# One more group of seven products in three FFN stages, and one pool for split weights and activations

## The chip, the core and the metric

The kernel runs on one core of a Trainium2 chip. The core has five engines with a queue each: TensorE (PE in the profile) multiplies matrices into PSUM, VectorE (DVE) and ScalarE (ACT) do elementwise work, GpSimd (POOL) does small work and issues some transfers, and SyncE (SP) issues the other transfers. An engine works its queue in order and waits on semaphores for the others. The metric is the device time of one execution in microseconds.

## The reference

The reference is a two-layer encoder over 256 tokens of width 1024, in float32. Each layer is a half FFN, an attention mixer and a second half FFN:

```
def swiglu(h, w_gate, w_up, w_down):
    return (jax.nn.silu(h @ w_gate) * (h @ w_up)) @ w_down
...
x = x + 0.5 * swiglu(rms_norm(x, ffn1_norm[l]), ffn1_w_gate[l], ffn1_w_up[l], ffn1_w_down[l])
h = rms_norm(x, mix_norm[l])
...                                # windowed and differential attention, output projection
x = x + 0.5 * swiglu(rms_norm(x, ffn2_norm[l]), ffn2_w_gate[l], ffn2_w_up[l], ffn2_w_down[l])
```

The FFN width is 2816. A last RMSNorm follows the second layer. This case is about the four FFNs, called stages 1 to 4 here.

## The kernel before, in words

**Precision.** Every float32 operand of a large product is split into a high part, rounded to the matmul's type, and a low part, the difference. A product is then three matmuls: high by high, low by high, high by low. ScalarE casts the high part and VectorE subtracts to get the low part, for weights (`emit_split`, L175) and for activations (`split`, L506). One weight step is a block of 512 rows by 512 columns, 1 MB, that lands in a `raw` buffer (6 of them); it is split in two halves of 128 x 1024 elements each, and each half fills two buffers tagged `w`.

**An FFN stage** (`ffn`, L567). The width 2816 is done in groups 0 to 4 of 512 columns and a tail of 256. A plain group multiplies the normed tokens `xs` with 512 columns of the gate and the up matrix (8 row blocks, 2 token blocks, 2 matrices, 3 matmuls: 96 matmuls of 128 x 512), then SiLU and the product give h (`gate`, `hidden`). The h of a group is transposed in the next group (`turn`, eight transposes, `hT`), where its two products with the down matrix (`down`, 24 matmuls each) also stand. Four PSUM banks hold the down sums (`accs`) from group 1 on; the other four go round among gate, up, transposes and products.

**Groups of seven products** (`by_seven`, L599). In groups 2, 3 and 4 of every stage, the gate and up products over two row halves and two token blocks are treated as a 2 x 2 by 2 x 2 block product and done with seven block products in place of eight (Strassen's scheme in Winograd's form). Each is 12 matmuls, so 84 in place of 96. They use sums of token blocks and sums of weight blocks. The token sums are made once a stage by `Norm.make_sums` (L332) from float copies of the normed tokens, `xg`, which `Norm.copies` (L322) writes from PSUM. It yields after each of four sums; each is an addition on VectorE (`tmp`), a cast on ScalarE and a subtraction on VectorE (tiles `q`, three times, and `v`). Two weight sums are accumulated by transfers that POOL issues (`gather`), two are made by VectorE (`plus`, two additions each on `raw`). The seven products, in their order in the code, are m1, m7, p2, p3, p5, p6 and p4; m7, p3, p5 and p6 take the token sums, and p3 takes the one that is made last. VectorE combines the products in seven operations on `tmp`, and two more make h.

**The order of the work.** Engines run in the order of the code in all of the FFN. Loads and splits of weights are put in ahead of their use by `ahead` (L211), called from `weights` (L232) and in the middle of each step by `Split.part`. The lookahead is HALVES = 6 halves, from 14 `w` buffers; activations have a pool of their own of 14 buffers (`s4`). In `make_sums` before, the sums are made in group 1, one after the gate, one after each of the two up steps, and one between the two down products.

**Around a stage.** The norm of the next stage begins while the last products of the one before still run; `Residual.late` (L557) finishes its statistics (`stats`: `ms`, then r by POOL, then `hr`) and makes the copies. In stage 1 `take_x` (L409) does that. `attention_constants` (L475), one transpose, a dozen small operations on VectorE and one exponential on ScalarE, is put in at the head of group 3 of stage 1 by `aside`; `final_gain` (L969), one transfer and one memset, at the head of group 3 of stage 4.

Of the kernel before, what the change touches and what calls it, by code (L numbers as in the profile page):

```python
# [21 lines left out]
NGRP = FF // 512  # L22
# [5 lines left out]
AHEAD = 10  # L28
N_RAW, N_W = 6, 14
N_S4 = 14  # L30
SEVEN = (2, 3, 4)


@with_exitstack
def trunk(ctx: ExitStack, tc: tile.TileContext, x, n1, g1, u1, d1, nm, w_in, sink,
# [124 lines left out]
    class Split:  # L160
# [5 lines left out]
        def part(self, k, c=slice(None), h=None):  # L166

            if h is None:
                h, k = divmod(k, 2)
            if h and not self.held:  # L170
                self.held = True
                ahead(2 * self.i + 1 + HALVES)
            return [t[:, k, c] for t in self.parts[h]]

    def emit_split(i, j):  # L175
# [4 lines left out]
        shape = (P, 8, P) if s.n == 256 else (P, 2, 512)  # L180
        hi, lo = [wp.tile(list(shape), F32R, tag="w", bufs=N_W, name=nm_("w")) for _ in range(2)]
        loaded[i].parts.append((hi, lo))
# [24 lines left out]

    HALVES = N_W // 2 - 1
    at = dict(use=0, dma=2, prep=2, split=4)
# [22 lines left out]
    def weights(less=0, held=False):  # L232

        i = at["use"]
        at["use"] += 1
        if i > 1:
            ahead(2 * i + HALVES - less)
        w = loaded[i]
        w.held = held
        return w  # L240

    for l in range(DEPTH):
        def ffn_specs(wg, wu, wd):
            down = lambda g, h: plain(wd[l], h * 512, 512, 4 * g, 4)
            for k0 in (0, 4):
                specs.extend(plain(w[l], 0, 512, k0, 4) for w in (wg, wu))
            for g in range(1, NGRP):
                downs = [down(g - 1, h) for h in range(2)]
                if g in SEVEN:
# [11 lines left out]

        ffn_specs(g1, u1, d1)
        wi = w_in[l]
# [19 lines left out]
        fine.update(range(mixed + 2, len(specs)))  # L283
        ffn_specs(g2, u2, d2)

# [3 lines left out]
    class Norm:  # L289


        def __init__(self, g0, sums=len(SEVEN) > 0):
# [39 lines left out]
        def make_sums(self):  # L332
# [5 lines left out]
            def make(x, y, op):  # L338
# [7 lines left out]
                return v  # L346

            s1 = make(b1, t1, ALU.subtract)
            yield
            s2 = make(s1, t0, ALU.add)  # L350
            yield
            make(t1, t0, ALU.subtract)
            yield
# [55 lines left out]
    def take_x(k):  # L409
# [14 lines left out]
        elif k == 2:  # L424
            ahead(7)
            for t in range(2):
                for h in range(2):
                    norm.squares(t, h * 512, 512)
            norm.stats()
            norm.copies()  # L430
            constants()
# [110 lines left out]
    class Residual:  # L542
# [14 lines left out]
        def late(self, k):  # L557
# [5 lines left out]
            elif k == 2:  # L563
                self.nxt.stats()
                self.nxt.copies()

    def ffn(norm, aside=None, before=None, final=False):  # L567
        def silu(out_, acc, t):
            act.activation(out_, acc, AF.Silu, scale=norm.r[:, t:t + 1])
# [28 lines left out]

        def by_seven(h, g):  # L599

# [64 lines left out]
        tokens(us, norm.xs, weights(), 4)  # L665
        h = hidden(g, us)
        for n in range(1, NGRP):
            sums = norm.make_sums() if n + 1 == min(SEVEN, default=0) else iter(())
            if n == 3 and aside is not None:
                aside()  # L670
            if n in SEVEN:
                h = by_seven(h, n)
                continue
            gs = [bank(), bank()]
            tokens(gs, norm.xs, weights(), 0)
            hT = turn(h, 2)
            tokens(gs, norm.xs, weights(), 4)
            g = gate(gs)
# [41 lines left out]
    def ffn_close(parts, nxt):  # L720
# [6 lines left out]
        tail(1)  # L727
        ahead(2 * at["use"] - 2 + HALVES)
        group(1, [(1, t) for t in range(2)])
# [326 lines left out]
```

## Time and profile before

| what | value |
|---|---|
| median of the runs shown | 944.5 us (944.03, 944.5, 947.19) |
| profiled execution, its own time | 946.16 us |
| its span, first to last instruction | 944.4 us |
| mean granted TensorE clock | 0.993 |
| PE busy | 924.9 us, 98% |
| DVE busy | 762.2 us, 81% |
| ACT busy | 582.2 us, 62% |
| POOL busy | 53.6 us, 6% |
| matmuls of 128 x 512 over a split weight, tokens in s | 2718, mean 394 ns from start to end |
| weight splits on DVE, 128 x 1024 | 336, 396.7 us |
| weight casts on ACT, 128 x 1024 | 336, 340.1 us |
| weight additions on DVE | 48, 56.5 us |
| accumulating transfers from POOL | 24 of 1 MB, median 10.7 us from issue to landing |

Matmuls overlap, so a mean of 394 ns is not the distance from one to the next. In the names of the profile, `w` is a split weight, `raw` a landed one, `s` an activation, `q` and `v` token sums in the FFN (and other tiles in attention), `tmp` the results of products and of SiLU. An arrow names who ended an idle time. All instructions carry the line of one helper, so groups are told apart by their tiles.

### The profile page before, as it was taken

Reading aid. Unit: us, or ns where it says so; the run is one execution under the profiler, and the core shown is the slowest. Engines: PE = TensorE matmul, PEld = TensorE weight load, DVE = VectorE, ACT = ScalarE, POOL = GpSimd, SP = SyncE. Lnnn points to the kernel's source line nnn. Section 1 sums busy time; section 2 is a strip of 40 time slices with the busy share of each in tenths; the row PEclk is TensorE's granted clock in tenths of the full one; section 3 lists DMA queues with packets and bytes.
Section 4 is the critical chain, followed back from the end, with each engine's and each line's share of the span. In section 5 each row is a group of like instructions: output and inputs, shape, how many; then the busy total and the mean of one; then the engine's idle time right before and its main releaser. Section 6 shows DMA issues by size and latency. Waiting matters only on the chain.

```text
span 944.4 us, 12947 instructions
## 1 busy us (share of the span) xinstructions
PE 924.9 (98%) x4796; PEld 783.5 (83%) x4796; DVE 762.2 (81%) x1066; ACT 582.2 (62%) x901; POOL 53.6 (6%) x73
## 2 busy tenths in 40 slices
PE   8999899999999999999999999999999999999997
PEld 6788688899898888887888888878999888888876
DVE  6679999869955678999866799996796556799993
ACT  6756576467735756675575566665676475575662
POOL 0500010000000000000000010000000000010001
PEclk9999899999999999999999999999999999999999
DMA  9986797836424875897658498886652348499821
GB/s 336 345 222 182 218 277 255 271 120 194 134 90 134 233 213 141 263 295 265 239 178 235 122 278 223 259 296 195 194 161 90 130 157 249 103 286 268 254 93 45
DMA packets 110895, 194.59 MB, mean 206 GB/s; under 512 B 3566, under 2 KB 31280, under 8 KB 110832
## 3 DMA queue, kind: packets, MB, share of 16 engines
q1 hardware_dynamic: 96816, 167.27, 52.2%
q0 software_dynamic: 12928, 25.46, 15.1%
q10 hardware_dynamic: 1088, 1.05, 0.3%
q8 instruction: 37, 0.61, 0.3%
q14 instruction: 26, 0.21, 0.1%
HBM read 192.71 MB, written 1.05 MB: 205 GB/s over the span
## 4 chain that ended last, share of the span: by engine, by line
PE 83%; DVE 7%; DMA 5%; issue 2%; ACT 2%; ACTq 0%; DVEq 0%; POOLq 0%; POOL 0%
PE ps L50 83%; DVE w L50 5%; DMA raw<-in_ffn_w_up_dram 3%; DVE tmp L50 1%; ACT w L50 1%; DMA raw<-in_ffn_w_gate_dram 1%; DMA xk<-in_x_dram 1%; DVE s L50 1%; DVE raw L50 0%; ACT s L50 0%; ACT junk L50 0%; ACT tmp L50 0%; ACT L50 0%; ACTq L50 0%; DVE xk L50 0%
## 5 line engine op out<-in xcount | busy, mean ns | idle before, releaser
L50 PE MATMUL ps<-w,s 128*128 128x512 f32 (+1 forms) x2754 | 645.4, 392 | 7.1 <-DVE tmp L50 3.5
L50 PEld LDWEIGHTS ps<-w,s 128*128 128x128 f32 x2754 | 514.0, 189 | 115.2 <-DVE tmp L50 4.8
L50 DVE TENSOR_TENSOR w<-raw,w 128x1024 fp32r<-128x1024 f32 (+1 forms) x440 | 464.1, 1094 | 86.9 <-ACT w L50 84.1
L50 ACT CAST w<-raw 128x1024 fp32r<-128x1024 f32 (+1 forms) x440 | 399.1, 949 | 189.7 <-PE ps L50 97.1
L50 PE MATMUL ps<-w,q 128*128 128x512 f32 x432 | 101.9, 389 | 0.0
L50 PEld LDWEIGHTS ps<-w,q 128*128 128x128 f32 x432 | 81.1, 188 | 16.8
L50 PE MATMUL ps<-s,w 128*128 128x256 f32 x672 | 84.0, 285 | 0.0
L50 PEld LDWEIGHTS ps<-s,w 128*128 128x128 f32 x672 | 81.7, 192 | 1.1
L50 DVE TENSOR_TENSOR raw<-raw,raw 128x1024 f32<-128x1024 f32 x48 | 56.5, 1218 | 0.0
L50 POOL DMA_DIRECT2D raw<-in_ffn_w_up_dram x24 | 31.0, 1293 | 364.4 <-DVE tmp L50 157.2
L50 DVE TENSOR_TENSOR s<-ps,s 128x512 fp32r<-128x512 f32 x48 | 31.0, 685 | 18.1 <-ACT s L50 18.1
L50 ACT ACTIVATE s<-ps,gcol 128x256 fp32r<-128x256 f32 (+1 forms) x80 | 31.3, 476 | 20.7 <-PE ps L50 20.7
L50 ACT CAST s<-ps 128x512 fp32r<-128x512 f32 x48 | 26.1, 594 | 28.1 <-PE ps L50 28.1
L50 PE MATMUL ps<-ident,s 128*128 128x128 f32 x304 | 39.9, 273 | 1.7 <-DVE s L50 1.7
L50 PEld LDWEIGHTS ps<-ident,s 128*128 128x128 f32 x304 | 35.0, 141 | 6.9 <-ACT w L50 1.8
L50 ACT ACTIVATE s<-s,negm 128x256 f32<-128x256 f32 x64 | 31.8, 500 | 6.6 <-DVE negm L50 6.6
L50 ACT ACTIVATE tmp<-tmp,r 128x512 f32<-128x512 f32 x24 | 17.3, 722 | 29.2 <-DVE tmp L50 29.2
L50 PE MATMUL ps<-w,v 128*128 128x512 f32 x144 | 34.6, 389 | 0.0
L50 PEld LDWEIGHTS ps<-w,v 128*128 128x128 f32 x144 | 27.2, 189 | 5.7
L50 DVE SCALAR_TENSOR_TENSOR s<-ps,gcol,s 128x256 fp32r<-128x256 f32 x48 | 20.3, 479 | 14.4 <-ACT s L50 14.3
L50 DVE TENSOR_TENSOR tmp<-ps,tmp 128x512 f32<-128x512 f32 x36 | 24.6, 684 | 0.0
L50 DVE TENSOR_TENSOR tmp<-tmp,ps 128x512 f32<-128x512 f32 x36 | 23.6, 683 | 0.4
(107 smaller groups left out, 407.0 us busy)
## 6 DMA issues: line engine op xcount, KB each, us to landing
raw<-in_ffn_w_down_dram SPq DMA_DIRECT2D x44, 1024.0 KB, 5.2
raw<-in_ffn_w_gate_dram SPq DMA_DIRECT2D x39, 1024.0 KB, 5.4
raw<-in_ffn_w_up_dram SPq DMA_DIRECT2D x39, 1024.0 KB, 5.1
raw<-in_ffn_w_up_dram POOLq DMA_DIRECT2D x24, 1024.0 KB, 10.7
raw<-in_w_in_dram SPq DMA_DIRECT2D x14, 1024.0 KB, 5.7
raw<-in_ffn_w_gate_dram SPq DMA_DIRECT2D x8, 512.0 KB, 6.7
raw<-in_ffn_w_up_dram SPq DMA_DIRECT2D x8, 512.0 KB, 7.7
raw<-in_w_in_dram SPq DMA_DIRECT2D x8, 512.0 KB, 5.1
```

The costliest lines, as they stand in the source:

```text
L50: ins = issue(*a, **k)
```

## The change

Six things change together. The groups done by seven products are (2, 3, 4) in stage 1 and (1, 2, 3, 4) in stages 2 to 4. Split weights and activations share one pool of 28 buffers. The lookahead is 8 halves in group 0, 1 and 2 of an FFN, 7 in group 3 and 6 in group 4, where three steps also put splits of later steps behind the combinations; it is 6 elsewhere. The copies `xg` are made in group 0 where group 1 is by seven, and otherwise behind the transposes of group 1. The token sums are made in another order (the one for m7 first): where group 1 is by seven, one after the gate and one after h of group 0, and two in group 1, behind the transposes. The attention constants go in between the two down products of the first plain group (group 1 of stage 1); `final_gain`, which stage 4 has no plain group for, goes behind group 4.

```diff
-N_RAW, N_W = 6, 14
-N_S4 = 14
-SEVEN = (2, 3, 4)
+N_RAW, N_S4 = 6, 28
+IN_FFN, IN_MIX = 8, 6
+
+SEVENS = (2, 3, 4), (1, 2, 3, 4)
...
-                ahead(2 * self.i + 1 + HALVES)
+                ahead(2 * self.i + 1 + look[0])
...
-        hi, lo = [wp.tile(list(shape), F32R, tag="w", bufs=N_W, name=nm_("w")) for _ in range(2)]
+        hi, lo = [s4.tile(list(shape), F32R, tag="s4", name=nm_("w")) for _ in range(2)]
...
-    HALVES = N_W // 2 - 1
+
+    look = [IN_MIX]
...
-            ahead(2 * i + HALVES - less)
+            ahead(2 * i + look[0] - less)
...
+            make(t1, t0, ALU.subtract)
+            yield
             s1 = make(b1, t1, ALU.subtract)
             yield
             s2 = make(s1, t0, ALU.add)
-            yield
-            make(t1, t0, ALU.subtract)
             yield
             make(b0, s2, ALU.subtract)
             yield
...
             norm.stats()
-            norm.copies()
             constants()
...
                 self.nxt.stats()
-                self.nxt.copies()
...
-            act.copy(m7, prod(norm.summed(2), weights(held=True)))
+            act.copy(m7, prod(norm.summed(0), weights(held=True)))
             hT = turn(h, 2)
+            for _ in sums:
+                pass
             p2 = prod(norm.quarter(0, 1), weights())
...
-            p5 = prod(norm.summed(0), weights())
-            p6 = prod(norm.summed(1), weights())
+            p5 = prod(norm.summed(1), weights())
+            late = g == NGRP - 1
+            p6 = prod(norm.summed(2), weights(look[0] - 5 if late else 0, late))
...
-            p4 = prod(norm.quarter(1, 1), weights())
+            p4 = prod(norm.quarter(1, 1), weights(look[0] - 4 if late else 0, late))
...
-            w = weights()
+            w = weights(look[0] - 3 if late else 0)
...
+        look[0] = IN_FFN
         before(0)
...
         before(2)
+        early_ = seven_[0] == 1
+        if early_:
+            norm.copies()
+        sums = norm.make_sums()
         tokens(gs, norm.xs, weights(), 4)
         g = gate(gs)
+        if early_:
+            next(sums)
         tokens(us, norm.xs, weights(), 4)
         h = hidden(g, us)
+        if early_:
+            next(sums)
         for n in range(1, NGRP):
-            sums = norm.make_sums() if n + 1 == min(SEVEN, default=0) else iter(())
-            if n == 3 and aside is not None:
-                aside()
-            if n in SEVEN:
-                h = by_seven(h, n)
+            if n in seven_:
+                look[0] = IN_FFN - max(0, n - 2)
+                h = by_seven(h, n, sums)
                 continue
             gs = [bank(), bank()]
             tokens(gs, norm.xs, weights(), 0)
             hT = turn(h, 2)
+            norm.copies()
...
                 if hh == 0:
                     next(sums, None)
+                    if aside is not None:
+                        aside()
+                        aside = None
+        if aside is not None:
+            aside()
...
         hE = []
+        look[0] = IN_MIX
         w = {0: weights()}
```

More of the change, by code (lines that the diff above doesn't have):

```diff
@@ L242, in trunk, with ffn_specs @@
     for l in range(DEPTH):
-        def ffn_specs(wg, wu, wd):
+        def ffn_specs(wg, wu, wd, seven_):
             down = lambda g, h: plain(wd[l], h * 512, 512, 4 * g, 4)
@@ L248, in ffn_specs @@
                 downs = [down(g - 1, h) for h in range(2)]
-                if g in SEVEN:
+                if g in seven_:
                     specs.extend(seven(wg[l], wu[l], g * 512, downs))
@@ L260, in ffn_specs @@
             specs.append(down(NGRP - 1, 1))
-        ffn_specs(g1, u1, d1)
+        ffn_specs(g1, u1, d1, SEVENS[l > 0])
         wi = w_in[l]
@@ L283, in trunk, with __init__ @@
         fine.update(range(mixed + 2, len(specs)))
-        ffn_specs(g2, u2, d2)
+        ffn_specs(g2, u2, d2, SEVENS[1])
     xk = const.tile([P, 2, D], F32, name="xk")
     class Norm:
-        def __init__(self, g0, sums=len(SEVEN) > 0):
+        def __init__(self, g0, sums=True):
             self.g0, self.xs, self.sums = g0, [], sums
@@ L564, in late @@
                 self.nxt.stats()
-                self.nxt.copies()
     def ffn(norm, aside=None, before=None, final=False):
+        seven_ = SEVENS[before is None]
         def silu(out_, acc, t):
@@ L597, in prod, with by_seven @@
             return acc
-        def by_seven(h, g):
+        def by_seven(h, g, sums):
             flat = lambda: tmp().rearrange("p a n -> p (a n)")
@@ L727, in ffn_close @@
         tail(1)
-        ahead(2 * at["use"] - 2 + HALVES)
+        ahead(2 * at["use"] - 2 + look[0])
         group(1, [(1, t) for t in range(2)])
```

## The prediction

> **What bounds the kernel now.** I read the page's parts 1 and 2 first, then the waits of TensorE, then TensorE and VectorE in order of time through one FFN stage. A stage is one FFN half of a layer; there are four, and in the trace they start near 6, 297, 477 and 758 us.
>
> ```profile
> PE 924.9 (98%) x4796; PEld 783.5 (83%) x4796; DVE 762.2 (81%) x1066; ACT 582.2 (62%) x901; POOL 53.6 (6%) x73
> ...
> PE   8999899999999999999999999999999999999997
> ...
> DVE  6679999869955678999866799996796556799993
> ```
>
> TensorE is busy nearly throughout, so a product that is left out shortens the span where nothing else is late. VectorE has four bands of nines: the seven-product groups 2 to 4 of each stage. The waits of TensorE are short:
>
> ```profile
> PE ps L50 <- DVE tmp L50: 3.5, 3, 1.2
> PE ps L50 <- ACT tmp L50: 3.5, 1, 3.5
> PE ps L50 <- DMA grow<-in_ffn_norm_dram: 3.4, 1, 3.4
> PE ps L50 <- DVE s L50: 1.7, 2, 1.4
> ```
>
> The first row is one wait of about 1.17 us after group 4 of each later stage; the second is in stage 1, where the attention constants stand in group 3. TensorE in order of time, stage 2:
>
> ```profile
> 359.21 1.03 PE L50 MATMUL ps<-ident,s 128*128 128x128 f32 x8
> ...
> 365.54 5.60 PE L50 MATMUL ps<-w,s 128*128 128x512 f32 x24
> 370.98 5.60 PE L50 MATMUL ps<-w,q 128*128 128x512 f32 x24
> ...
> 390.02 1.03 PE L50 MATMUL ps<-ident,s 128*128 128x128 f32 x8
> ```
>
> 24 matmuls take 370.98 - 365.54 = 5.44 us, 0.2267 each. From the transposes of one seven-product group to those of the next is 30.81 us. VectorE beside it:
>
> ```profile
> 347.98 0.69 DVE L50 TENSOR_TENSOR tmp<-s,tmp 128x512 f32<-128x512 f32 x1
> 349.35 0.69 DVE L50 TENSOR_TENSOR v<-tmp,v 128x512 fp32r<-128x512 f32 x1 [0.69 <-ACT v L50]
> ...
> 372.91 6.90 DVE L50 TENSOR_TENSOR w<-raw,w 128x1024 fp32r<-128x1024 f32 x6
> ...
> 392.97 1.28 DVE L50 TENSOR_TENSOR s<-ps,s 128x512 fp32r<-128x512 f32 x2
> ...
> 425.19 1.28 DVE L50 TENSOR_TENSOR s<-ps,s 128x512 fp32r<-128x512 f32 x2
> ```
>
> One weight split costs VectorE 6.90/6 = 1.15 us. A token sum costs 350.04 - 347.98 = 2.06 us, because the split behind it waits 0.69 for ScalarE's half. VectorE's own round is 32.22 us, 1.4 more than TensorE's: it falls behind in each such group, and only slack from groups 0 and 1 carries it. The windows table gives the clock at the two longer stops:
>
> ```profile
> 40.00:42.00 2.00, 2.00 (x6) 1.52 (x6) 2.00 (x4) 1.00 (x2) 0.93 (x1) 0.50 1.06 402
> ...
> 111.00:113.00 2.00, 2.00 (x6) 1.52 (x6) 2.00 (x4) 2.00 (x4) 0.00 (x0) 0.50 0.00 0
> ```
>
> The seventh entry is the granted clock. After 1.70 us of stops near 37.8 it is 0.50 for 3.4 us (1.7 lost); after the 3.52 us stop at 105.8 for 6.8 us, of which 5.3 lie behind the stop (2.65 lost). After the 1.17 us stops it stays at 1.00.
>
> **The change, part by part.**
>
> *Products.* Group 1 of stages 2 to 4 goes from 96 gate/up matmuls to 84: 12 x 0.2267 = 2.72 us less on TensorE per stage, all on the path. VectorE gets 6 splits (6.9), 4 weight additions (4.7) and 7 combinations (4.6) more per stage.
>
> *Sums moved before group 1.* These must now be ready inside group 1. Work it out on stage 2's own times. Group 0 ends on TensorE at 303.78 + 72 x 0.2267 = 320.1 with or without the change. In group 1 then come products m1 and m7 (2.72 each), eight transposes (0.79) and p2 (2.72), so p3 is due at 329.05. It needs the fourth sum. VectorE's list up to there, by rows of before: hr ends at 312.34; two splits end at 315.6 (as now, 313.28 + 2.36); the first sum waits for ScalarE, which has its table load and the SiLU pair until 316.9, and ends at 318.2; two splits end at 320.8; the two hidden halves take 1.32, to 322.1; the second sum 2.06, to 324.2; two splits, whose casts stand behind that sum's cast on ScalarE, 2.6, to 326.8; one split behind the copy of m1 and its own cast 1.3, to 328.1; the two splits of hT 1.24, to 329.3; the third and fourth sum 2.06 each, to 333.3. TensorE can do the first matmul of p3 on ScalarE's half at 332.5 and stops again for VectorE's. The new stop is 4.0 us. Without any wait for ScalarE but those inside the sums it would be 320.1 + 1.32 + 2.06 + 3 x 1.15 + 1.24 + 4.0 = 332.1, a stop of 3.0; with one more cast (0.98) ahead of a sum, 5.0. I take 4.0, as each of its steps has a row of this stage. In stage 3 no table load stands there (1.28 us on ScalarE), and the same list ends about 0.5 earlier: 3.5. Stage 4 is as stage 2.
>
> *The clock behind that stop.* The nearest rows are the stops of 1.70 (1.7 lost) and 3.52 (2.65 lost). How long half clock lasts hangs on where the stop falls against windows of 3.4 us. Sliding a stop of 4 us over them, with half clock whenever more than about 1.5 us of a window is idle (1.17 did nothing; the clock fell at 107.8, and the 1.5 us of the stop after that, to 109.3, kept it down), gives 0.95 to 2.65 and 1.8 on average. I take 1.8. The Trainium skill, TensorE: Matmul & The Clock Gate, section "Why this matters for your kernels", warns of gaps over about 3 us and ties half clock to one idle window of about 3.4 us; by that rule the stop of 1.70 us would have cost nothing, and the trace disagrees.
>
> *Behind it.* The stop gives VectorE time. From 333.3 its next round (18 splits, 4 additions, 7 combinations, 2 halves: 32.22 - 1.24 = 31.0) brings hT of group 2 to 364.3, where TensorE ends its transposes at 350.81 + 5.8 + 5.44 + 0.79 = 362.85: 1.4 late, against 0.5 now. Groups 3 and 4 split one half less before their combinations (lookahead 7, then 6), so VectorE's round is 31.07 against 30.82 and the lateness stays near 1.7. h of group 3 is done at 423.0, its transposes are due at 423.7. In group 4 three more splits go behind the combinations, and the stop of 1.17 us goes. The stage ends with about 0.7 us of cover.
>
> *Accumulating transfers.* Two more on POOL's queue per stage; the second stands ahead of r there. It waits for the first split (308.7) and takes 1.29 to issue: done at 310.0, before ms at 311.3. Its 10.7 us to landing end near 321, its split is due at 326.8. If it were late, the splits of p5 would be, 15 us before p5 is due. Nothing is added. SP's queue has the same transfers with two swapped.
>
> *Stage 1.* It keeps (2, 3, 4). The constants move into group 1: VectorE needs 107.4 - 103.9 = 3.5 us for them, and idles 0.26 + 0.62 + 1.49 + 0.84 + 0.99 = 4.2 there. The next product is on splits made before them. So the stop of 3.52 and its 2.65 of clock go: -6.2. The copies of the normed tokens move behind the first transposes of group 1, so four banks stay taken, and group 1 cannot start at 30.7 but when the SiLU pair frees two (33.4; two more casts stand ahead of it). That stop of 2.75 swallows today's 1.70 behind it; the transposes end at 39.75 instead of 39.14. The clock loss is about the same. +0.6. Stage 1: -5.6 (-7 to -3.5). Lookahead in its other groups only helps VectorE. The one pool holds 27 of 28 buffers at the fullest point, so casts do not wait longer there. final_gain moves behind group 4 of stage 4, some 15 us ahead of its use: nothing.
>
> **Sum.** Stages 2 and 4: -2.72 - 1.17 + 4.0 + 1.8 = +1.9 each; stage 3: +1.4; stage 1: -5.6. Together -0.4 us. The profiled execution took 946.16 us (span 944.4, 1.8 around it), 1.7 above the median of 944.5; the difference is taken from the median: 944.1 us. Bounds of the stop (3.0 to 5.0), the clock (0.95 to 2.65) and stage 1 give -8 to +9 if all lie on one side, and 940 to 948 for this case.
>
> **The rivals.**
>
> No clock loss: the stops come as worked out, but the clock stays at 1.00, as after 1.17 us. 944.1 - 3 x 1.8 = 938.7. For it: windows are free to fall well. Against it: 1.70 us was enough once. (It is also what the Trainium skill, TensorE: Matmul & The Clock Gate, section "Why this matters for your kernels", gives if read strictly: a stop of 4.0 us holds a whole 3.4 us window about one time in five, so 944.1 - 0.8 x 5.4 = 939.8 by it.)
>
> No stop: the sums are ready at p3. Then 3 x (3.8 + 1.8) = 16.8 go, and the old end stops (3.5) come back, as VectorE gets no rest: 944.1 - 16.8 + 3.5 = 930.8. Against it stands the chain of 12 us on VectorE from h to the fourth sum, where TensorE has 8.95.
>
> Slower: VectorE sets the pace in groups 2 to 4. Place: the transposes of groups 3, 4 and the tail wait for h. It decides once hT of group 2 comes over 2.1 us after its transposes (0.7 more than my 1.4); then each of the rounds at 32.22 shows: 2.2 at group 4 and 1.4 at the tail, 3.6 a stage, 944.1 + 10.8 = 954.9. For it: VectorE at 99% in these bands, and ScalarE waited 18 us in all for accumulated weights; against: the shrinking lookahead.
>
> The constants still stop stage 1: the 6.2 stay, 950.3. VectorE's 4.2 us of idle against 3.5 needed is thin, but three products' worth of splits lie ahead.
>
> **How the numbers follow.** The worked case has 0.44 (0.30 within 0.3%, 0.09 faster, 0.05 slower), no clock loss 0.22, no stop 0.08, VectorE's pace 0.17, the constants 0.07; of the 0.02 left half goes to either side. A change under 0.3%, 2.8 us, cannot be told from none here. Faster 0.09 + 0.22 + 0.08 + 0.01 = 0.40, same 0.30, slower 0.05 + 0.17 + 0.07 + 0.01 = 0.30. The likeliest case says 944.1, written 944. The range leaves out the no-stop case and the worse half of VectorE's pace: 936 to 952.
>
> **What would show it.** Right: in stages 2 to 4 one TensorE wait each of 3 to 5 us in the first seven-product group, at products that read the tile v, ended by the split of v; half clock behind it; no wait for DVE tmp behind group 4; no 3.5 us wait near 106 us, and one of near 3 us at 31 us for ACT tmp. Wrong: no wait at v; TensorE waits at transposes of groups 3 and 4; casts waiting for accumulated weights several us at a time.

## The result, and the profile after

The changed kernel takes 954.24 us (median of 4 runs, 953.58 to 955.27) where the kernel before takes 944.26 beside it: a ratio of 1.0108, 95% interval 1.0088 to 1.0129. The change makes the kernel 1.1% slower. The forecast was 944 with a range of 936 to 952, and the time lies above it. It is close to that of the third rival, VectorE setting the pace (954.9), but in part by luck: that rival's sum has 16.0 us lost in the later stages and 5.6 gained in stage 1, where 9.4 and 2.7 were measured. The profiled execution took 953.9 us, its span is 952.0 (before: 946.16 and 944.4).

The page of the changed kernel, busy time and the slices of TensorE and VectorE:

```profile
PE 920.7 (97%) x4760; PEld 776.2 (82%) x4760; DVE 803.4 (84%) x1117; ACT 593.8 (62%) x925; POOL 58.8 (6%) x79
...
PE   7998999999999899899998999999999998999997
...
DVE  6769999869866799999778999996697678999993
```

TensorE has 36 matmuls fewer, three times twelve, as the change says, and is 4 us less busy, yet its share falls from 98% to 97%: the span grew by stops. VectorE is 41.2 us busier. The waits of TensorE in the changed kernel (us in total, times, longest):

```profile
PE ps L51 <- ACT v L51: 8.3, 3, 2.9
PE ps L51 <- DVE s L51: 4.6, 10, 0.8
...
PE ps L51 <- ACT tmp L51: 3.4, 1, 3.4
PE ps L51 <- DVE tmp L51: 2.2, 4, 0.7
```

The first row is the new stop at product p3, once in each later stage. The second and fourth are many short stops, nearly all in groups 2 to 4 of the later stages, that were not there before. The third, the stop behind the attention constants, was to go and is still there. TensorE in order of time, groups 1 and 2 of stage 2 (start, duration; in brackets the idle time before and what ended it):

```profile
324.23 2.99 PE L51 MATMUL ps<-w,s 128*128 128x512 f32 x12
330.18 0.51 PE L51 MATMUL ps<-w,v 128*128 128x512 f32 x1 [2.95 <-ACT v L51]
330.90 2.79 PE L51 MATMUL ps<-w,v 128*128 128x512 f32 x11 [0.22 <-DVE v L51]
...
358.01 1.03 PE L51 MATMUL ps<-ident,s 128*128 128x128 f32 x8
358.80 2.98 PE L51 MATMUL ps<-w,s 128*128 128x512 f32 x12
...
384.28 3.01 PE L51 MATMUL ps<-w,s 128*128 128x512 f32 x12 [0.74 <-DVE tmp L51]
387.88 2.96 PE L51 MATMUL ps<-w,q 128*128 128x512 f32 x12 [0.59 <-DVE tmp L51]
391.62 0.33 PE L51 MATMUL ps<-ident,s 128*128 128x128 f32 x1 [0.78 <-DVE s L51]
392.29 0.98 PE L51 MATMUL ps<-ident,s 128*128 128x128 f32 x7 [0.34 <-DVE s L51]
```

p3 was due at 324.23 + 12 x 0.2267 = 326.95; its second matmul, due at 327.18, runs at 330.90: a stop of 3.72. At the head of group 3 stand four stops; its transposes follow those of group 2 after 34.2 us instead of 30.8. VectorE beside it:

```profile
328.79 0.69 DVE L51 TENSOR_TENSOR tmp<-s,tmp 128x512 f32<-128x512 f32 x1
330.16 0.69 DVE L51 TENSOR_TENSOR v<-tmp,v 128x512 fp32r<-128x512 f32 x1 [0.68 <-ACT v L51]
...
362.06 1.28 DVE L51 TENSOR_TENSOR s<-ps,s 128x512 fp32r<-128x512 f32 x2
...
381.17 2.36 DVE L51 TENSOR_TENSOR w<-raw,w 128x1024 fp32r<-128x1024 f32 x2 [2.41 <-ACT w L51]
```

It starts to split hT of group 2 at 362.06, where TensorE's transposes ended at 358.80: 3.26 late. The last line waits for ScalarE, which itself waits 3.16 us at 380.09 for a weight that POOL's transfer accumulates.

What each stage takes, by the ends of its transposes in TensorE's order of time. For stage 1 it is the time at which the tail's end; for the others the distance from those of group 1 to those of the tail. With four groups of seven and no stop that distance would be 126.0 - 2.7 = 123.3, since it is 126.0 in the run below with three groups and no stop in these stages.

| kernel | median, us | stage 1 | stage 2 | stage 3 | stage 4 |
|---|---|---|---|---|---|
| before | 944.3 | 173.5 | 127.7 | 127.8 | 127.9 |
| changed | 954.2 | 170.8 | 131.3 | 130.9 | 130.7 |

So stage 1 gains 2.7, the later ones lose 3.6, 3.1 and 2.7; 0.5 and 0.4 more go in the two stretches that have the attention in them.

### The profile page after: what moved, and what is told of

Its sections match the earlier page's. It is cut to its first block, busy times and chain, and to the rows that moved or that the text cites. A ratio compares the mean times of both kernels' runs of the same rounds, so it can differ in the third digit from the quotient of the medians.

```text
span 952.0 us, 12724 instructions
## 1 busy us (share of the span) xinstructions
PE 920.7 (97%) x4760; PEld 776.2 (82%) x4760; DVE 803.4 (84%) x1117; ACT 593.8 (62%) x925; POOL 58.8 (6%) x79
## 4 chain that ended last, share of the span: by engine, by line
PE 56%; DVE 18%; DMA 15%; issue 5%; ACT 4%; POOLq 0%; ACTq 0%; POOL 0%; DVEq 0%
PE ps L51 56%; DMA raw<-in_ffn_w_up_dram 15%; DVE w L51 11%; DVE tmp L51 4%; ACT w L51 2%; DVE s L51 2%; DVE raw L51 1%; ACT q L51 1%; DMA xk<-in_x_dram 1%; ACT tmp L51 0%; ACT s L51 0%; ACT L51 0%; ACT v L51 0%; DVE q L51 0%; DVE distA L51 0%
## 5 line engine op out<-in xcount | busy, mean ns | idle before, releaser
L51 PE MATMUL ps<-w,s 128*128 128x512 f32 (+1 forms) x2574 | 602.6, 392 | 4.1 <-ACT tmp L51 3.4
L51 PEld LDWEIGHTS ps<-w,s 128*128 128x128 f32 x2574 | 479.5, 189 | 102.7 <-ACT tmp L51 3.8
L51 DVE TENSOR_TENSOR w<-raw,w 128x1024 fp32r<-128x1024 f32 (+1 forms) x458 | 481.5, 1098 | 39.4 <-ACT w L51 38.6
L51 ACT CAST w<-raw 128x1024 fp32r<-128x1024 f32 (+1 forms) x458 | 409.8, 951 | 122.6 <-DVE raw L51 94.1
L51 PE MATMUL ps<-w,q 128*128 128x512 f32 x540 | 127.6, 390 | 1.5 <-DVE tmp L51 1.5
L51 PEld LDWEIGHTS ps<-w,q 128*128 128x128 f32 x540 | 101.1, 188 | 23.6 <-issue 2.7
L51 POOL DMA_DIRECT2D raw<-in_ffn_w_up_dram x30 | 38.8, 1294 | 523.4 <-DVE w L51 242.6
L51 DVE TENSOR_TENSOR raw<-raw,raw 128x1024 f32<-128x1024 f32 x60 | 70.6, 1217 | 0.0
L51 ACT ACTIVATE s<-ps,gcol 128x256 fp32r<-128x256 f32 (+1 forms) x80 | 31.4, 480 | 49.4 <-PE ps L51 49.4
L51 PE MATMUL ps<-w,v 128*128 128x512 f32 x180 | 46.0, 403 | 9.0 <-ACT v L51 8.3
L51 ACT CAST q<-tmp 128x512 fp32r<-128x512 f32 x20 | 12.4, 620 | 35.4 <-DVE tmp L51 35.4
L51 DVE SCALAR_TENSOR_TENSOR s<-ps,gcol,s 128x256 fp32r<-128x256 f32 x48 | 20.3, 477 | 13.7 <-ACT s L51 13.6
## 6 DMA issues: line engine op xcount, KB each, us to landing
raw<-in_ffn_w_up_dram POOLq DMA_DIRECT2D x30, 1024.0 KB, 12.3
```

The source lines that it names most:

```text
L51: ins = issue(*a, **k)
```

## The experiments

The theory after the result: (A) each later stage is short of VectorE time from group 1 on, so the stop at p3 and the stops in groups 2 to 4 are one shortage in two places, and in stage 1 the longer lookahead takes the buffers that hold up the constants. The rivals: late weights (the accumulated ones) make the stops in groups 2 to 4; the lookahead or the one pool costs the time everywhere; the place of p3 alone does.

**Group 1 back to eight products.**

```diff
-SEVENS = (2, 3, 4), (1, 2, 3, 4)
+SEVENS = (2, 3, 4), (2, 3, 4)
```

> The changed kernel, but groups 2 to 4 alone by seven products in every stage, as before; one pool, lookahead by place and the moved constants stay. It tells what group 1 costs from what the rest costs. Theory A (group 1 is what costs: its late fourth sum, 3.2 to 3.7 us of stop in each of stages 2 to 4, and VectorE's lateness behind it): stages 2 to 4 fall to the before time or 1.2 us under it each (no stop behind group 4), stage 1 stays 2.7 us under before: 944.3 - 2.7 - 3.5 = 938, at most 942. Theory B (the lookahead of 8 puts splits whose accumulated weights have not landed ahead of VectorE's combinations, with or without group 1): stops of 1 to 4 us stay in groups 2 to 4, and the time is 945 to 950.

Measured: 940.68 us, ratio to before 0.9968 (0.9955 to 0.998). The later stages take 126.0 each, with no stop on TensorE in any of them. So seven products in group 1 cost 954.2 - 940.7 = 13.5 us, and all the rest of the change together gains. Stage 1 still has its stop for the constants (4.11 us near 76 us, half clock for 6.8 us around it); the tail's transposes end at 172.6.

**Lookahead 6 throughout, four groups of seven.**

```diff
-IN_FFN, IN_MIX = 8, 6
+IN_FFN, IN_MIX = 6, 6
...
-                look[0] = IN_FFN - max(0, n - 2)
+                look[0] = IN_FFN
```

> The changed kernel with a lookahead of 6 halves in all groups of all stages (8, 8, 8, 7, 6 in the changed kernel). Theory A (VectorE has more work than time, wherever its splits stand): the stops at the fourth sum stay near 3.5 us, the stops in groups 2 to 4 stay at 3 to 4 us a stage in sum or grow; only the wait of 6.3 us for buffers in group 1 of stage 1 and the 3.4 us stop behind it may go, 5 us: 949 to 955. Theory B (splits of weights that have not landed stand ahead of the combinations): the waits of ScalarE for accumulated weights no longer stop VectorE (2.4 us in group 2 of stage 2), the stops in groups 2 to 4 fall below 1 us a stage: 940 to 945.

Measured: 945.12 us, 1.0007 (0.9992 to 1.0023). Stage 1 has lost the stop for the constants, and its tail comes at 165.4, 5.4 earlier than in the changed kernel. The later stages take 129.9, 129.8 and 130.8, which is 1.4 and 1.1 less than in the changed kernel and 0.1 more. So the longer lookahead is what costs stage 1.

The time is at the upper end of what theory B had said (940 to 945) and below theory A's (949 to 955), and the stops side with B too: TensorE's waits in groups 2 to 4 are 0.54, 0.85 and 0.99 us a stage, below the 1 us that B had said, where the changed kernel has 2.78, 1.73 and 2.00. VectorE's waits for casts in groups 2 and 3 fall from 2.75, 2.91 and 1.74 us a stage to 0, 0.2 and 1.0. So late weights behind the longer lookahead do carry a part of the loss. How large a part is not clear, as half clock stood behind all three stops at p3 here and behind one in the changed kernel; in stage 3, which has it in both, the longer lookahead costs 1.1. Most of the loss stays: 129.9 against 126.0 with three groups.

**The same for the head of stage 1 alone.** Lookahead 6 in groups 0 and 1 of stage 1, 8 as before the edit everywhere else:

```diff
-        look[0] = IN_FFN
+        look[0] = IN_FFN if seven_[0] == 1 or norm.g0 else IN_MIX
```

> Lookahead 6 in place of 8 in groups 0 and 1 of stage 1 alone, the rest as in the changed kernel. If the buffers taken by the lookahead hold up the constants in stage 1 (the 6.29 us wait of a cast, then the 3.36 us stop with half clock), the stop at 76 us goes, the tail transposes of stage 1 end near 165.4 us as in the run with lookahead 6 everywhere, and the time falls by 5.4 us, to 949 (947 to 951), while stages 2 to 4 keep their stops (130.5 to 131.5 us from the transposes of group 1 to those of the tail). If it was the lookahead in stages 2 to 4 that cost most, the time stays above 951.5.

Measured: 950.56 us, 1.0069 (1.0055 to 1.0082). ScalarE in stage 1, first in the changed kernel, then here:

```profile
57.80 2.00 ACT L51 CAST w<-raw 128x1024 fp32r<-128x1024 f32 x2 [6.29 <-PE ps L51]
...
71.50 0.20 ACT L51 ACTIVATE lex<-lsum 128x4 f32<-128x4 f32 x1 [2.14 <-DVE lsum L51]
71.61 3.87 ACT L51 CAST w<-raw 128x1024 fp32r<-128x1024 f32 x4
75.39 0.57 ACT L51 COPY tmp<-ps 128x512 f32<-128x512 f32 x1
```

```profile
64.86 0.21 ACT L51 ACTIVATE lex<-lsum 128x4 f32<-128x4 f32 x1 [2.14 <-DVE lsum L51]
64.97 5.79 ACT L51 CAST w<-raw 128x1024 fp32r<-128x1024 f32 x6
70.67 0.57 ACT L51 COPY tmp<-ps 128x512 f32<-128x512 f32 x1
```

In the changed kernel a cast waits 6.29 us in group 1 for TensorE to free a buffer. Token sums and constants queue behind it, the exponential of the constants (`lex`) comes at 71.50, and four casts stand between it and the copy of m1, which frees the bank that TensorE needs for p2. With two halves less ahead the same copy is done 4.7 earlier and TensorE does not stop. The tail of stage 1 ends at 166.4, 4.4 earlier. The time fell by 3.7, not 5.4: the later stages took 130.0, 131.0 and 131.4 and had half clock behind two of their three stops at p3, where the profiled execution of the changed kernel had it behind one.

**p3 behind the first product with the down matrix**, in group 1 of the later stages, so that the sum has 5.4 us more (the weights load in that order too):

```diff
-            p3 = prod(norm.summed(3), weights())
-            silu(g0, g0, 0)
-            down(hT, g - 1, 0, weights())
+            if g == 1:
+                silu(g0, g0, 0)
+                down(hT, g - 1, 0, weights())
+                p3 = prod(norm.summed(3), weights())
+            else:
+                p3 = prod(norm.summed(3), weights())
+                silu(g0, g0, 0)
+                down(hT, g - 1, 0, weights())
```

> The changed kernel, but in group 1 of stages 2 to 4 the product p3, which needs the last token sum, stands behind the first down product (24 matmuls, 5.4 us), with its weights loaded and split in that order. The work is the same. Theory A1 (the stops add up): the stops at p3 (3.7, 3.2, 3.7 and 1.4 of clock) go and nothing takes their place: 954.2 - 12 = 942. Theory A2 (VectorE's pace): p3 no longer stops, but VectorE is then 3.5 us later against TensorE at the transposes of group 2, and the stops at banks and at h in groups 2 to 4 grow by about that: 950 to 954.

Measured: 959.68 us, 1.0168 (1.0152 to 1.0184), 5.4 slower than the changed kernel and outside what either theory had said (942, or 950 to 954). The stop at v is gone. TensorE in stage 2 of this run:

```profile
342.82 0.73 PE L51 MATMUL ps<-w,s 128*128 128x512 f32 x2 [0.80 <-ACT w L51]
344.08 8.00 PE L51 MATMUL ps<-w,s 128*128 128x512 f32 x34 [0.53 <-DVE w L51]
352.72 2.97 PE L51 MATMUL ps<-w,s 128*128 128x512 f32 x12 [0.64 <-DVE tmp L51]
356.32 3.00 PE L51 MATMUL ps<-w,q 128*128 128x512 f32 x12 [0.62 <-DVE tmp L51]
360.06 0.33 PE L51 MATMUL ps<-ident,s 128*128 128x128 f32 x1 [0.74 <-DVE s L51]
```

The waits stand now at weight splits in group 1 and at banks and transposes in group 2, one group earlier than in the changed kernel, and the stages take 131.9, 132.8 and 132.6. Giving the sum time did not give VectorE time. It took some: VectorE's round from hT of group 1 to hT of group 2 is 38.3 us in place of 36.45, as VectorE waits 1.79 (at 342.80) for a cast that stands on ScalarE behind the SiLU of g0. The later stages lose 0.6, 1.9 and 1.9 against the changed kernel; the other 1.2 lie in stage 1, which the order does not touch and where half clock lasted 6.8 us in place of 3.4.

**Without the weight additions** of VectorE (`plus` emptied; two of the seven products then use incomplete weight sums):

```diff
-                for h in (0, 2):
-                    x_, t_ = [raws[i][:, h:h + 2] for i in (x, to)]
-                    dve.tensor_tensor(t_, t_, x_, op=ALU.add)
+                pass
```

> The changed kernel without VectorE's additions on weights (60 instructions of 1.2 us, 4.7 us in each seven-product group); the products that should have the sums of three and four weight blocks are made with the sum of two, so the output is another. It takes work from VectorE alone, and the waits of casts for these additions. If VectorE's pace makes the stops in groups 2 to 4, they go in all of stages 2 to 4 (4.3, 2.9 and 3.6 us), while the stops at the fourth sum stay at 3 to 4 us: 943 to 945. If late accumulated weights make them, VectorE's waits behind casts stay or grow and the stops stay above 2 us a stage: 948 to 953.

Measured: 945.26 us, 1.0014 (1.0 to 1.0027), 0.3 above the range I had given; 128.4, 128.1 and 127.0 in the later stages. TensorE in stage 2, from p3 on:

```profile
331.08 4.85 PE L51 MATMUL ps<-w,v 128*128 128x512 f32 x12 [2.94 <-ACT v L51]
...
360.28 1.03 PE L51 MATMUL ps<-ident,s 128*128 128x128 f32 x8
...
391.09 1.04 PE L51 MATMUL ps<-ident,s 128*128 128x128 f32 x8
```

The stop at p3 is as before the edit, and behind it there is none: 30.81 us from transposes to transposes. The accumulating transfers are all still made, so late transfers alone do not stop TensorE in groups 2 to 4: it takes VectorE's list, which is 4.7 us a group shorter here. In groups 2 and 3 of stage 2 VectorE now waits 3.9 us of each round and is 0.5 late at hT, where it was 1.9 to 3.6 late in the later stages of the changed kernel. The edit also takes away the waits of casts for these additions, so it relieves somewhat more than VectorE's time. What this run leaves in the later stages is the stop at p3 and half clock behind two of them; in stage 1 the constants still stop TensorE, for 4.60 us.

**Both: no additions, p3 behind the down product** (and lookahead 6 at the head of stage 1):

```diff
-                for h in (0, 2):
-                    x_, t_ = [raws[i][:, h:h + 2] for i in (x, to)]
-                    dve.tensor_tensor(t_, t_, x_, op=ALU.add)
+                pass
...
+            if g == 1:
+                silu(g0, g0, 0)
+                down(hT, g - 1, 0, weights())
+                p3 = prod(norm.summed(3), weights())
...
```

> Lookahead 6 at the head of stage 1, no weight additions on VectorE (the products use the sums without them, so the output differs), and p3 of group 1 behind the first product with the down matrix. If the stop at p3 and the stops behind it are one shortage of VectorE, this order now gains the whole stop, since a round is 27.5 us on VectorE against TensorE's 30.8: the later stages take 124 to 125 us (128 without the additions and with the old order, 132 with this order and the additions), and the time is 950.6 less 3 x 6.5, so 931 (929 to 934). If the weights of p3, loaded behind those of the down product, are late in this order by themselves, a stop of over 1.5 us stands at p3 and the time is above 936.

Measured: 926.89 us, 0.982 (0.9806 to 0.9835), with 123.9, 123.4 and 123.9 in the later stages, within 0.6 of no stop at all. The waits of TensorE there:

```profile
PE ps L51 <- DMA grow<-in_ffn_norm_dram: 3.3, 1, 3.3
PE ps L51 <- DMA xk<-in_x_dram: 1.5, 2, 1.1
PE ps L51 <- DVE s L51: 0.7, 2, 0.3
PE ps L51 <- ACT tmp L51: 0.4, 1, 0.4
```

The first two are the start of the kernel. The order that cost the later stages 4.4 us with the additions gains the whole stop without them. Two stops with causes of their own would have let the order gain in both runs; one shortage of VectorE in two places lets it gain only where VectorE has time left behind it, and that is what came. The wait of 1.79 for a cast is here as well (at 331.64) and costs nothing. It came out 4 us better than I had said, 2 us below my range: I had left 0.7 to 1.7 us a stage for remaining stops, and there were hardly any.

**Token sums without VectorE** (each by two copies on ScalarE, so the sums' values are not right; lookahead 6 at the head of stage 1):

```diff
-                dve.tensor_tensor(v, x, y, op=op)
...
-                act.copy(sm[:, :, 0:P], v)
-                dve.tensor_tensor(sm[:, :, P:S], v, f(sm[:, :, 0:P]), op=ALU.subtract)
+                act.copy(sm[:, :, 0:P], x)
+                act.copy(sm[:, :, P:S], y)
```

> Lookahead 6 at the head of stage 1, and the token sums made by two copies on ScalarE each, without the addition and the subtraction on VectorE (the output differs). It takes 4 x 2.06 = 8.2 us off VectorE's list ahead of p3 in each stage. If that list sets the stop at p3, the stop goes and VectorE is some 4.5 us further ahead in group 2, so that the stops in groups 2 to 4 shrink to 1 us a stage or none: stages of 124 to 125.5 us, 931 to 934. If ScalarE's casts set it, the stop stays above 1.5 us, and the time is above 940.

Measured: 940.14 us, 0.996 (0.9945 to 0.9975): 10.4 us under the run with lookahead 6 at the head of stage 1 alone, where 17 to 20 were expected. The time falls into the other branch of the expectation (above 940), but the sign of that branch, a stop at p3, is not there. The stop is gone, so the sums' list on VectorE sets it. The stops behind it are not. VectorE in stage 2 of this run:

```profile
320.44 1.29 DVE L51 TENSOR_TENSOR s<-ps,s 128x512 fp32r<-128x512 f32 x2 [0.97 <-ACT s L51]
323.95 1.23 DVE L51 TENSOR_TENSOR w<-raw,w 128x1024 fp32r<-128x1024 f32 x1 [2.22 <-ACT w L51]
...
354.89 1.28 DVE L51 TENSOR_TENSOR s<-ps,s 128x512 fp32r<-128x512 f32 x2
```

From hT of group 1 to hT of group 2 it takes 34.45 us, its round of 32.2 and a wait of 2.22 for a cast, where TensorE takes 31.3; hT of group 2 is 354.89 - 351.23 = 3.7 late. My expectation credited VectorE with the 8.2 us of all four sums less the stop that had hidden them. But only two of them, 4.1 us, stand behind hT of group 1; ahead of it VectorE waits for TensorE's transposes in any case. Of these 4.1 the wait of 2.22 takes back half: the cast starts at 322.85, behind the four copies that now make these two sums on ScalarE. VectorE's round fell by 2.0 (36.45 to 34.45), TensorE's by 3.3 (34.57 to 31.31), and 127.2, 128.7 and 127.9 us remain.

**Half of the additions on GpSimd** (with lookahead 6 at the head of stage 1):

```diff
-                for h in (0, 2):
+                for e, h in ((dve, 0), (pool, 2)):
                     x_, t_ = [raws[i][:, h:h + 2] for i in (x, to)]
-                    dve.tensor_tensor(t_, t_, x_, op=ALU.add)
+                    e.tensor_tensor(t_, t_, x_, op=ALU.add)
```

> As the first, and the second half of each weight addition on GpSimd in place of VectorE (half of 4.7 us a group: 2.3 us less, so a round of 29.9 us against TensorE's 30.8). If VectorE's pace makes the stops in groups 2 to 4, they go as they did without the additions (stages of 127 to 128.4 us in place of 131), the stop at p3 stays near 3 us, and the time is 949 - 3 x 2.5 = 941 (939 to 944). If late weights make them, GpSimd's slower additions make it worse: over 950, with casts waiting for raw longer than 3 us.

Measured: 1046.42 us, 1.1086 (1.1071 to 1.1101). It does not say anything against VectorE's pace, since it did not relieve VectorE. GpSimd and VectorE in stage 1 of this run:

```profile
77.40 3.32 POOL L51 TENSOR_TENSOR raw<-raw,raw 128x1024 f32<-128x1024 f32 x1 [22.14 <-DVE w L51]
83.14 3.31 POOL L51 TENSOR_TENSOR raw<-raw,raw 128x1024 f32<-128x1024 f32 x1 [2.43 <-DVE w L51]
86.39 1.30 POOL L51 DMA_DIRECT2D raw<-in_ffn_w_up_dram  x1
```

```profile
79.57 3.49 DVE L51 TENSOR_TENSOR w<-raw,w 128x1024 fp32r<-128x1024 f32 x2 [1.12 <-ACT w L51]
...
104.22 2.35 DVE L51 TENSOR_TENSOR w<-raw,w 128x1024 fp32r<-128x1024 f32 x2
```

Two things went wrong. The accumulating transfer, issued at 78.45 without this edit, stands on POOL's queue behind both additions and is issued at 86.39; ScalarE then waits 6.17 us for it at 99.53, and TensorE 6.61 at 103.72. And two splits that run beside the GpSimd addition take 3.49 us, two that don't 2.35: VectorE gets back the 1.2 us of an addition and loses 1.1. (The Trainium skill, SBUF — State Buffer, section "Who interferes with whom", says that an operation of VectorE with two SBUF inputs contends with one of GpSimd that reads SBUF, and that the port pair which they share is an exclusive lock. The rows agree: the split starts at 79.57, GpSimd's addition ends at 80.72, and the extra time is 1.14.)

**The same with p3 behind the down product:**

```diff
-                for h in (0, 2):
+                for e, h in ((dve, 0), (pool, 2)):
...
+            if g == 1:
+                silu(g0, g0, 0)
+                down(hT, g - 1, 0, weights())
+                p3 = prod(norm.summed(3), weights())
...
```

> As the third, and product p3 of group 1 behind the first product with the down matrix. If the stop at p3 and the stops in groups 2 to 4 are one shortage of VectorE, relieved by 2.3 us a group, this order now gains most of the stop: 936 to 940. If the shortage is not relieved, the stop only moves behind group 1 as it did before: within 1.5 us of the third run or slower.

Measured: 1045.63 us, 1.1076 (1.1061 to 1.1091). It stands within 1.5 us of the run before, but with GpSimd's delays of 7 to 8 us a group over everything it tells nothing about the order of p3.

**Three groups of seven, lookahead 6 at the head of stage 1:**

```diff
-SEVENS = (2, 3, 4), (1, 2, 3, 4)
+SEVENS = (2, 3, 4), (2, 3, 4)
...
-        look[0] = IN_FFN
+        look[0] = IN_FFN if seven_[0] == 1 or norm.g0 else IN_MIX
```

> The same, and seven products in groups 2 to 4 only in all stages. If the two losses are independent (group 1 by seven in stages 2 to 4, buffers in stage 1), the run with three groups, 940.7 us, loses the rest of its stops in stage 1 too: its tail transposes came at 172.6 us against 165.4, so 933.5 (932 to 936), faster than both kernels by over 1 percent, with 126.0 us in each later stage. If the rest hangs together otherwise (buffers short again in group 2 of stage 1), 937 to 941.

Measured: 936.38 us, 0.9918 (0.9905 to 0.9932). The later stages take 126.0, 126.4 and 126.0, the tail of stage 1 comes at 167.1, where I had said 165.4. It is faster than both kernels, and 0.4 us above the range I had given: with lookahead 8 from group 2 on, stage 1 keeps stops of 0.82 at 72 and 1.1 at 103.

**Three groups of seven, lookahead 6 throughout:**

```diff
-IN_FFN, IN_MIX = 8, 6
+IN_FFN, IN_MIX = 6, 6
-SEVENS = (2, 3, 4), (1, 2, 3, 4)
+SEVENS = (2, 3, 4), (2, 3, 4)
...
-                look[0] = IN_FFN - max(0, n - 2)
+                look[0] = IN_FFN
```

> Seven products in groups 2 to 4 only, and lookahead 6 throughout, so that of the change only the one pool, the places of the sums, copies, constants and final_gain are left. If the longer lookahead is what takes the end stops of 1.17 us away, they come back and the time is 936.4 + 3 x 1.2 = 940 (939 to 942), with later stages of 127.2 us or more. If the move of the constants is nearly all of the gain, it is the same as with lookahead 8, 935 to 938.

Measured: 934.67 us, 0.9898 (0.9882 to 0.9915), 0.3 below the range of the second case: the fastest of the kernels that leave no work out, 1.0% faster than before. The waits of TensorE:

```profile
PE ps L51 <- DMA grow<-in_ffn_norm_dram: 3.4, 1, 3.4
PE ps L51 <- DMA xk<-in_x_dram: 1.3, 2, 1.0
PE ps L51 <- DVE s L51: 1.0, 3, 0.3
```

The stops of 1.17 us at the end of the later stages did not come back, so it is not the longer lookahead that takes them away. Stage 1 ends its tail's transposes at 164.9, 8.6 before the kernel before; the later stages take 127.2, 126.3 and 126.1. Group 4 still puts three steps' splits behind the combinations here, and the sums, the copies and the pool are those of the change; which of these removes the end stops was not separated.

**The kernel before, with the constants alone moved** to between the down products of group 1:

```diff
             if n == 3 and aside is not None:
                 aside()
+                aside = None
...
                 if hh == 0:
                     next(sums, None)
+                    if aside is not None and not final:
+                        aside()
+                        aside = None
```

> The kernel before, with the attention constants alone moved, from the head of group 3 of stage 1 to between the two products with the down matrix of group 1. By the step of the prediction that prices them, the stop of 3.52 us near 106 us and the 2.65 us of half clock go: 944 - 6.2 = 938 (936.5 to 939.5), with the tail transposes of stage 1 at 167.3 us in place of 173.5, and the later stages as they were (127.8 us). If the constants only stop TensorE elsewhere, as in the changed kernel, the tail transposes come at 170 us or later and the time is above 941.

Measured: 939.99 us, 0.996 (0.9947 to 0.9973). In the profiles the step is as priced: the tail's transposes end at 167.4 in place of 173.5, the stop of 3.52 is gone and a stop of 1.20 for DVE tmp stands at 161.75 instead, as in the later stages. By the medians it gains 3.4, 0.5 short of the range I had given. The profiled execution of before, from which the 2.65 us of clock were read, lay 1.9 above the median, with a mean granted clock of 0.993, where the runs beside this one had 0.994 to 0.998, most of them 0.996: most executions had less half clock. That the stop of the constants is where they had less is likely, but no trace shows it.

All runs without GpSimd, side by side:

| kernel | median, us | stage 1 | stage 2 | stage 3 | stage 4 |
|---|---|---|---|---|---|
| four groups, lookahead 6 | 945.1 | 165.4 | 129.9 | 129.8 | 130.8 |
| four groups, 6 at the head of stage 1 | 950.6 | 166.4 | 130.0 | 131.0 | 131.4 |
| four groups, p3 behind down | 959.7 | 172.0 | 131.9 | 132.8 | 132.6 |
| four groups, no additions | 945.3 | 171.7 | 128.4 | 128.1 | 127.0 |
| four groups, free sums | 940.1 | 166.5 | 127.2 | 128.7 | 127.9 |
| four groups, no additions, p3 behind down | 926.9 | 165.4 | 123.9 | 123.4 | 123.9 |
| three groups, lookahead 8 | 940.7 | 172.6 | 126.0 | 126.0 | 126.0 |
| three groups, 6 at the head of stage 1 | 936.4 | 167.1 | 126.0 | 126.4 | 126.0 |
| three groups, lookahead 6 | 934.7 | 164.9 | 127.2 | 126.3 | 126.1 |
| before, constants moved | 940.0 | 167.4 | 127.9 | 127.7 | 127.7 |

## Why the prediction was wrong

*Products: right.* There are 36 matmuls less, worth 8.2 us at 0.2267 each. TensorE's busy time fell by 4.2 only; it also counts half clock and the first matmuls behind stops, and was not taken apart. Where nothing stops TensorE the gain shows: from transposes to transposes group 1 of stage 3 takes 30.93 in the run without additions and with p3 moved, and 33.54 with three groups, 2.6 less where 2.72 was forecast.

*The stop at p3: right.* Forecast 4.0, 3.5 and 4.0; measured 3.72, 3.21 and 3.71. The list of VectorE ahead of it held in order and in length, and the run with free sums shows that it is this list.

*The clock behind it: over-sized.* Forecast 1.8 each, 5.4 in all. In the profiled execution half clock came behind one of the three stops. The granted clock (the seventh entry) in the changed kernel, in the stop of stage 2, behind it, and behind that of stage 3:

```profile
328.00:330.00 2.00, 0.00 (x0) 0.00 (x0) 1.29 (x2) 0.64 (x2) 0.00 (x0) 1.00 0.39 150
331.00:335.00 4.00, 4.00 (x18) 3.31 (x19) 3.90 (x4) 1.50 (x3) 0.41 (x1) 1.00 0.75 114
...
514.00:517.00 3.00, 3.00 (x8) 2.40 (x9) 2.96 (x3) 0.57 (x2) 0.29 (x1) 0.52 0.65 97
```

Over the four kernels without GpSimd's additions that have the stop at p3 it came behind 8 of 12 such stops, 3.4 us long each time, so 1.7 lost or nothing: 1.1 on average. By the rule that the prediction cites beside it (the Trainium skill, TensorE: Matmul & The Clock Gate, section "Why this matters for your kernels") it would have come one time in five for a stop of 4.0 us, an estimate; the measurement lies between that and the forecast.

*Behind it: this is the step that failed.* It said that hT of group 2 comes 1.4 late and that no stops follow. VectorE came to hT when it said: with stage 2 starting 2.2 earlier than before, the split at 362.06 stands for 364.3. TensorE did not: without half clock it ended its transposes at 358.80 + 2.2 = 361.0, not 362.85. So hT was 3.26 late, past the 2.1 from which the third rival decides; in stage 4, also without half clock, 3.57, and in stage 3, with it, 1.85. Stops followed, at the heads of groups 3 and 4; the rival had priced them at group 4 and the tail. The end stops of 1.17 did go, and the loss that took their place is larger: the stages lost 3.6, 3.1 and 2.7 where the sum had 1.9, 1.4 and 1.9.

The error was to let the loss of clock buy VectorE time in one term and, in the rival, to price stops as if they came on top. They do not add: what TensorE doesn't lose at p3 or to the clock, it loses behind, since VectorE's list sets the end of both. Six stages show it, those of the changed kernel and of the run with lookahead 6 at the head of stage 1, which are alike from stage 2 on: with half clock behind the stop they took 130.0, 130.9 and 131.4, without it 131.3, 131.0 and 130.7. The runs with p3 moved, with the additions away and with both show the same from three sides.

*Accumulating transfers: "nothing is added" failed too.* In groups 2 and 3 of the later stages VectorE's own list takes 31.1 to 31.4, near the 31.07 forecast. But its rounds from hT to hT lasted 33.49 and 31.69 in stage 2, 32.35 and 32.91 in stage 3, 32.56 and 31.70 in stage 4. In them are 2.41, 2.58 and 1.40 us a stage of waits for casts that themselves wait for accumulated weights, as here:

```profile
380.09 4.84 ACT L51 CAST w<-raw 128x1024 fp32r<-128x1024 f32 x5 [3.16 <-DMA raw<-in_ffn_w_up_dram]
```

The transfers landed 12.3 us after their issue in the median, where the sum had 10.7. In stage 3, where hT of group 2 came less than 2.1 late, the stops of 0.33 and 1.40 follow mostly from these waits (an estimate: without them VectorE would have come to hT some 0.4 past the 2.5 at which TensorE stops there). VectorE's waits for casts are smaller where it is less late (0.8, 1.2 and 0.5 with three groups of seven and the same lookahead, and they stop nothing) and with lookahead 6 (0, 0.2 and 1.0). How the loss of a stage divides between the list and the late weights was not separated. TensorE's waits at the transposes of groups 3 and 4, and casts that wait 2.0 to 3.2 us for accumulated weights, are signs of being wrong that the prediction names.

*Stage 1: failed.* Forecast -5.6, measured -2.7. The step that failed is "The one pool holds 27 of 28 buffers at the fullest point, so casts do not wait longer there": a cast waited 6.29 us in group 1, and the constants' stop of 3.36 with 1.7 of clock stood at group 2 instead of group 3. The fourth rival had about the right price for it (the 6.2 stay) but the wrong cause, VectorE's thin idle time; with lookahead 6 the same idle time is enough. From the transposes of group 2 to the tail the changed kernel gains only 0.8. The other 1.9 come ahead of them, where +0.6 was forecast: the stop near 31 us for the banks was not seen in the changed kernel (three of the runs show 0.41 to 0.91 there), and the stops near 37.8 of the kernel before went, together with the half clock behind them.

*The base.* The sum was made on an execution 1.7 above the median of 944.5 that it starts from; the changed kernel's profiled execution lay 0.3 below its median. Of the miss of 10.1 us, 2.0 are this; 4.2 are the later stages, 2.9 stage 1, and 0.9 the stretches between.

## What to carry to other kernels

When a helper engine's round (36.45 us in group 1, 31.1 and the waits for late weights behind it) is longer than the main engine's (30.8), moving work earlier only moves the stop: price the helper's whole list to the end of the stage, and don't add stops that the same list sets, nor count a stop as rest for it twice. A group that saves the main engine 2.7 us and costs the helper 13.7 pays only where the helper has that slack: here seven products in group 1 cost 13.5 us. Without the 4.7 us of additions a group, with p3 moved and lookahead 6 at the head of stage 1, the kernel took 926.9, but its sums are then incomplete. And a deeper lookahead in a shared pool is a queue in front of everything that allocates behind it: look where small urgent work stands in it.

## What the runs showed of the hardware

- Stops of 3.2 to 3.7 us on TensorE at p3 were followed by half clock for 3.4 us in 8 of 12 cases and by none in 4, in the same code; stops of 1.16 to 1.20 us by none in 7 of 7 (before, and before with the constants moved, in the later stages and stage 1). By an estimate from these rows one such stop at p3 costs 0 or 1.7 us of clock, so two executions of one kernel can differ by that much a stop.
- An addition of 128 x 1024 takes 1.22 us on VectorE and 3.31 on GpSimd beside VectorE's work, and splits of VectorE that overlap it take 1.14 longer: moving it gave VectorE back next to nothing.
